# Two second key products in one PSUM bank, squared by one instruction

## The chip, the cores and the metric

The kernel runs on one core of one Trainium2 chip. The metric is the device time of one execution in microseconds (us). Five engines work side by side, each through its own queue in order: TensorE (PE in the profile; PEld are its weight loads), VectorE (DVE), ScalarE (ACT), GpSimd (POOL) and SyncE (SP, which issues DMAs). Engines wait for each other by semaphores only. Matmul results go to PSUM, which has eight banks of 512 fp32 values per partition; ACT and DVE read them there, POOL does not.

## The reference, cut to what matters

One inference step of a one-layer decoder: 1024 prompt tokens, and 8 sequences that decode 8 tokens each against a paged cache of 8192 positions. The change lies in the attention of the decoding tokens over the cached pages. For each page the cached latent `c` is projected to keys and values, and the keys are normalised per head:

```python
def latent_to_kv(ckv, krope, w_kvup, g_kn):
    kv = (ckv @ w_kvup).reshape(ckv.shape[:-1] + (MLA_HEADS, MLA_NOPE + MLA_V))
    k_nope = rmsnorm(kv[..., :MLA_NOPE], g_kn)
```

`rmsnorm` needs, for each cached position and each of the 8 heads, the sum of the squares of 64 key values. The scores, a running softmax over the pages and the sum over the values follow. Everything else of the layer (projections, gated linear attention, prompt attention, output projection, convolutional MLP, per-layer embedding) is "dense" work of the prompt.

## The kernel before, in words

**Cached pages.** Each sequence's 8192 positions are 8 blocks of 1024, so 64 blocks in all. A block is 8 tiles of 128 positions; the first block of a sequence has a ninth tile for the new tokens. `stage_load` (line 462) gathers a block by two indirect DMAs on POOL. `turn` (line 515) transposes four tiles on PE into one bank and splits them into a high and a low part on ACT (line 116) and DVE (line 117): `cTh`, `cTl`. A key is never kept: `main` (line 543) multiplies a tile by the key half of the projection only to get its squares, and the raw scores come from the same product, since the projection matrix `mv` carries 64 more columns with the query absorbed. `main` is called once per group of four tiles (and once for the ninth).

**The two products of a tile.** The 512 key columns and the 64 score columns don't fit one bank, so a tile has a first product of 320 columns (256 key columns, 64 scores) and a second of 256 columns. Each product is three fp32r matmuls (`mm3`, lines 138 to 141: high by high, high by low, low by high) into its own bank `ks` of the pool `psK`, which has three banks. ACT squares the 256 key columns out of the bank into `csq` (line 560) and, after a first product, copies the 64 scores to `sn` (line 562). When two tiles are squared, DVE sums their squares per head into `css` (line 565). The bank of a product is thus used again by the third product after it, once ACT has read it.

**What follows a block.** `stage_b` (line 580) turns the sums into inverse norms (ACT, DVE), scales the scores on POOL and takes their maxima; `stage_c1` (line 606) turns the maxima on PE (`mt`), takes exponentials on ACT and splits them into `phl`; `stage_pv` (line 638) multiplies them by the cached latents (`cpv`). These run one and two blocks behind `main`, as `cache_stream` (line 678) lays out: per block two steps, each ended by a `yield`.

**The order of the work.** The loop of lines 1602 to 1614 interleaves the cache stream with the dense work: each cache step is due 4.4 us times a factor `PACE` of the current dense part after the one before, each dense step names its own cost, and the one that is behind goes next. This gives the program order. From it, the queue of each engine is fixed when the program is built: the builder follows the program with its own estimates of durations and lets the first instruction in program order that it believes ready go next. What is estimated wrongly becomes a wait on the chip, with all that stands behind it in that queue. When the dense work has ended (`"fill" in z`), output-projection units (`wo_unit`, line 1424) are placed by hand between the pairs of tiles by `place` (line 574), and `behind` (line 570) keeps PE in program order there. The pool `psK` is closed after the cached pages; the MLP and the rest (from line 1616) don't use it.

Of the kernel before, what the change touches and what calls it, by code (L numbers as in the profile page):

```python
# [8 lines left out]
F32 = mybir.dt.float32  # L9
# [3 lines left out]
AF = mybir.ActivationFunctionType  # L13
ALU = mybir.AluOpType
AX = mybir.AxisListType
# [3 lines left out]
P = 128  # L19
# [26 lines left out]
def step_kernel(ctx: ExitStack, tc: tile.TileContext, A):  # L46
    nc = tc.nc
    pe, act, dve, pool, sp = nc.tensor, nc.scalar, nc.vector, nc.gpsimd, nc.sync
# [89 lines left out]
    def mm3(ps, ah, al, bh, bl, first=True, last=True):  # L138
        pe.matmul(ps, ah, bh, start=first, stop=False)  # L139
        pe.matmul(ps, ah, bl, start=False, stop=False)  # L140
        return pe.matmul(ps, al, bh, start=False, stop=last)  # L141
# [41 lines left out]
    psK = ph1.enter_context(tc.tile_pool(name="psK", bufs=3, space=PSUM))  # L183
    cp = ph1.enter_context(tc.tile_pool(name="cp", bufs=1, side="right"))
# [10 lines left out]
    def cst(shape, dt, name):  # L195
        return cp.tile(shape, dt, name=name, tag=name)

    oL = ctile([P, H, R], F32, "oTm")
    z = {}

    mv = [[cst([P, 576], F32R, f"mv{i}{s}") for s in "hl"] for i in range(2)]
# [341 lines left out]
    def main(o, g0):  # L543
        buf = o.b % 2
        if g0 == 0:
            o.sn = cp.tile([P, 9, 64], F32, tag="sn", name="sn", bufs=3)
            o.ss = cp.tile([P, 9, 8], F32, tag="css", name="css", bufs=2)
        gn = min(4, o.nt - g0)
        cTh, cTl = turned_c[groups.index((o.n, g0))]
        for i in range(gn):  # L550
            if i % 2 == 0:
                sq2 = cp.tile([P, 2, 512], F32, tag="csq", name="csq", bufs=2)
            sq = sq2[:, i % 2]
            for f in range(2):
                ks = psK.tile([P, 512], F32, tag="k", name="ks")
                w = 256 if f else 320
                mh, ml = (m[:, f * 320:f * 320 + w] for m in mv[buf])
                with behind():
                    z["chain"] = mm3(ks[:, :w], cTh[:, i, :], cTl[:, i, :], mh, ml).ins
                act.activation(sq[:, f * 256:f * 256 + 256], ks[:, 0:256], AF.Square)  # L560
                if f == 0:
                    act.copy(o.sn[:, g0 + i, :], ks[:, 256:320])  # L562
            if i % 2 or i == gn - 1:
                n = i % 2 + 1
                dve.tensor_reduce(o.ss[:, g0 + i + 1 - n:g0 + i + 1, :].rearrange("p i h -> p (i h)"),  # L565
                                  sq2[:, :n].rearrange("p i (h n) -> p (i h) n", n=64), AX.X, ALU.add)
                if "fill" in z and n == 2:
                    place()

    def behind():  # L570

        return tc.issue_after(z["chain"]) if "fill" in z and "chain" in z else nullcontext()

    def place():

        z["slot"] += 1
        if z["slot"] > 6 and z["slot"] % 8 and z["units"] < 49:
            fill(1)
# [99 lines left out]
    def cache_stream():  # L678
# [7 lines left out]
        for n in range(N + 2):  # L686
            z["block"] = n
            if n + 2 < N:
                blk[n + 2] = stage_load(*todo[n + 2], n + 2)
            if n < N:  # L690
                pre(blk, blk[n], 4)
                main(blk[n], 0)
            if 0 <= n - 2:
                stage_pv(blk[n - 2])
            if 0 <= n - 1 < N:
                stage_b(blk[n - 1])
            yield
            if n < N:
                if blk[n].nt == 9:
                    pre(blk, blk[n], 8)  # L700
                    main(blk[n], 4)
                    pre(blk, blk[n + 1], 0)
                    main(blk[n], 8)
                else:
                    if n + 1 < N:
                        pre(blk, blk[n + 1], 0)
                    main(blk[n], 4)
            if 0 <= n - 1 < N:
                stage_c1(blk[n - 1])
            if 0 <= n - 2:  # L710
                stage_c2(blk.pop(n - 2))
            yield
# [881 lines left out]
    def fill(n):  # L1594
        for _ in range(n):
            z["units"] += next(z["fill"], done) is None
# [5 lines left out]
    while live_c or live_d:  # L1602
# [4 lines left out]
        else:  # L1607
            w = next(dn, done)
# [268 lines left out]
    h, hs = z["h"], z["hs"]  # L1877
# [336 lines left out]
```

## Time and profile before

| what | us |
|---|---|
| time, median of three executions | 2253.16 |
| lowest, highest | 2251.01, 2255.33 |
| span of the profiled execution (first to last instruction) | 2250.3 |
| PE busy in it | 2147.8 (95%) |
| ACT busy | 1357.9 (60%) |
| DVE busy | 1681.4 (75%) |
| POOL busy | 1356.9 (60%) |

The profile is of one execution of its own; its time is told as its span, which leaves out what lies before the first and after the last instruction. A group's row reads: line, engine, operation, output<-input, shape, count, busy time, mean duration in ns, idle time of the engine just before these instructions and what ended it. A row of the waits reads: who waited, for whom, us in total, times, the longest. PE and PEld are one queue: a matmul's weight load goes ahead of it, so a product that waits for its bank shows as idle time before its weight load, its first matmul, or both.

### The profile page before, as it was taken

To read this page: it belongs to the slowest core of one execution; us is meant where nothing else is said; L and a number is where in the kernel's file an instruction comes from. 1 tells how busy PE (TensorE), PEld (TensorE's weight loads), DVE (VectorE), ACT (ScalarE), POOL (GpSimd) and SP (SyncE) were. 2 spreads that over 40 slices of the span, in tenths; PEclk is the share of its full clock that TensorE was granted. 3 is DMA by queue.
4 is the path that set the end of the run, shared out by engine and by line. 5 is a ranking of instruction groups with operands and counts; after the bars stand their busy time and mean duration, and the time that the engine had idled before them with its cause. 6 is when DMAs were issued, how large, how long until landed. Compare 5 with 4: busy or idle time off the path is not lost.

```text
span 2250.3 us, 38434 instructions
## 1 busy us (share of the span) xinstructions
PE 2147.8 (95%) x13459; PEld 1937.9 (86%) x13459; DVE 1681.4 (75%) x2490; ACT 1357.9 (60%) x3692; POOL 1356.9 (60%) x1395
## 2 busy tenths in 40 slices
PE   7999989999999999998999988999999999998999
PEld 6889978878888888887888867999999997786899
DVE  4675776467788888886978888888888877966632
ACT  5666766777778898886777775433333334334521
POOL 5675677577777777676455467656566643589000
PEclk9899999999999999999999998999999999999999
DMA  5343244413242222213322222322222228456321
GB/s 184 115 134 102 84 126 147 139 55 88 83 122 59 60 66 74 66 41 100 122 66 78 63 104 62 113 94 90 94 94 96 93 70 291 154 193 206 112 76 37
DMA packets 204547, 233.60 MB, mean 104 GB/s; under 512 B 42430, under 2 KB 146339, under 8 KB 204355
## 3 DMA queue, kind: packets, MB, share of 16 engines
q1 hardware_dynamic: 190691, 184.21, 26.1%
q0 software_dynamic: 12432, 42.48, 6.2%
q10 hardware_dynamic: 1232, 4.46, 0.5%
q8 instruction: 108, 1.77, 0.3%
q14 instruction: 84, 0.69, 0.1%
HBM read 188.52 MB, written 42.52 MB: 103 GB/s over the span
## 4 chain that ended last, share of the span: by engine, by line
PE 71%; DVE 9%; POOL 6%; DMA 5%; ACT 5%; issue 3%; SPq 0%; POOLq 0%; ACTq 0%; DVEq 0%
PE ps_gu L140 7%; PE ps_gu L141 7%; PE ps_gu L139 7%; PE ks L139 4%; PE ks L141 4%; PE ks L140 4%; PE cpv L645 2%; PE ctp L522 2%; DMA raw<-ffn_w_down 2%; PE ps_lt L278 2%; PE ps_pj L139 2%; DVE css L565 1%; PE ps_pj L140 1%; PE ps_pj L141 1%; PE ps_pg L140 1%
## 5 line engine op out<-in xcount | busy, mean ns | idle before, releaser
L560 ACT ACTIVATE csq<-ks 128x256 f32<-128x256 f32 x1040 | 392.4, 400 | 85.6 <-PE ks L141 76.6
L565 DVE TENSOR_REDUCE css<-csq 128x16 f32<-128x1024 f32 (+1 forms) x264 | 315.7, 1197 | 62.9 <-ACT csq L560 59.8
L116 ACT CAST wh<-st 128x512 fp32r<-128x512 f32 x176 | 108.3, 619 | 183.3 <-PE ps_gu L140 163.8
L139 PE MATMUL ks<-mv1h,cTh 128*128 128x320 f32 (+1 forms) x520 | 169.5, 328 | 8.4 <-ACT sn L562 3.6
L139 PE MATMUL ks<-mv0h,cTh 128*128 128x320 f32 (+1 forms) x520 | 170.8, 330 | 6.9 <-ACT csq L560 3.0
L604 POOL TENSOR_TENSOR chl<-craw,chl 128x1024 fp32r<-128x1024 f32 x64 | 141.2, 2206 | 57.3 <-ACT chl L603 56.7
L140 PE MATMUL ks<-mv1l,cTh 128*128 128x320 f32 (+1 forms) x520 | 153.3, 297 | 0.0
L140 PE MATMUL ks<-mv0l,cTh 128*128 128x320 f32 (+1 forms) x520 | 152.1, 294 | 0.0
L141 PE MATMUL ks<-mv0h,cTl 128*128 128x320 f32 (+1 forms) x520 | 147.8, 297 | 0.9 <-DVE cTl L117 0.8
L630 POOL TENSOR_TENSOR phl<-sn,phl 128x512 fp32r<-128x512 f32 (+1 forms) x64 | 84.8, 1326 | 105.0 <-ACT phl L629 104.6
L141 PE MATMUL ks<-mv1h,cTl 128*128 128x320 f32 (+1 forms) x520 | 147.9, 298 | 0.0
L117 DVE TENSOR_TENSOR wl<-st,wh 128x512 fp32r<-128x512 f32 x132 | 119.0, 903 | 29.0 <-ACT wh L116 29.0
L140 PE MATMUL ps_dn<-o 128*128 128x512 f32 x308 | 125.6, 408 | 12.1 <-DVE o L117 12.0
L117 POOL TENSOR_TENSOR wl<-st,wh 128x512 fp32r<-128x512 f32 x44 | 69.1, 1574 | 104.3 <-ACT wh L116 104.3
L139 PE MATMUL ps_dn<-o 128*128 128x512 f32 x308 | 119.6, 399 | 4.5 <-ACT o L116 4.5
L141 PE MATMUL ps_dn<-o 128*128 128x512 f32 x308 | 123.8, 402 | 0.0
L117 DVE TENSOR_TENSOR cTl<-ctp,cTh 128x512 fp32r<-128x512 f32 (+1 forms) x136 | 90.0, 662 | 37.3 <-ACT cTh L116 36.3
L1317 POOL TENSOR_TENSOR pl<-p,ph 128x512 fp32r<-128x512 f32 (+1 forms) x96 | 97.4, 1019 | 33.0 <-DVE ph L1316 23.2
L562 ACT COPY sn<-ks 128x64 f32<-128x64 f32 x520 | 117.1, 225 | 0.0
L139 PEld LDWEIGHTS ks<-mv1h,cTh 128*128 128x128 f32 x520 | 98.8, 190 | 20.7 <-ACT sn L562 7.4
L139 PEld LDWEIGHTS ks<-mv0h,cTh 128*128 128x128 f32 x520 | 97.9, 188 | 20.8 <-ACT sn L562 7.0
L139 PE MATMUL ps_gu<-xrh,wh 128*128 128x320 f32 x352 | 108.6, 309 | 0.9 <-ACT xrh L116 0.9
(675 smaller groups left out, 8019.0 us busy)
## 6 DMA issues: line engine op xcount, KB each, us to landing
raw<-ds SPq DMA_DIRECT2D x77, 256.0 KB
raw<-ffn_w_down SPq DMA_DIRECT2D x66, 256.0 KB
stage<-w_in SPq DMA_DIRECT2D x48, 256.0 KB
st<-ffn_w_gate SPq DMA_DIRECT2D x44, 256.0 KB
st<-ffn_w_up SPq DMA_DIRECT2D x44, 256.0 KB
wr<-ffn_w_down SPq DMA_DIRECT2D x44, 256.0 KB
ds<-cv SPq DMA_DIRECT2D x21, 512.0 KB
oraw<-doT SPq DMA_DIRECT2D x16, 256.0 KB
```

The costliest lines, as they stand in the source:

```text
L116: act.copy(hi, src)
L117: (lo_eng or dve).tensor_tensor(lo, src, hi.bitcast(F32), ALU.subtract)
L139: pe.matmul(ps, ah, bh, start=first, stop=False)
L140: pe.matmul(ps, ah, bl, start=False, stop=False)
L141: return pe.matmul(ps, al, bh, start=False, stop=last)
L278: pe.matmul(ps, x, w, start=first, stop=last)
L560: act.activation(sq[:, f * 256:f * 256 + 256], ks[:, 0:256], AF.Square)
L562: act.copy(o.sn[:, g0 + i, :], ks[:, 256:320])
L565: dve.tensor_reduce(o.ss[:, g0 + i + 1 - n:g0 + i + 1, :].rearrange("p i h -> p (i h)"), sq2[:, :n].rearrange("p i (h n) -> p (i h) n", n= ...
L604: pool.tensor_tensor(ch[:, c0:c1, 128:256], src, ch[:, c0:c1, 0:128].bitcast(F32), ALU.subtract)
L630: pool.tensor_tensor(phl[:, :nt, 64:128], sb, phl[:, :nt, 0:64].bitcast(F32), ALU.subtract)
L1317: pool.tensor_tensor(pl[:, c0:], p[:, c0:], ph[:, c0:].bitcast(F32), ALU.subtract)
```

## The change

The second products of two neighbouring tiles go into the two halves of one bank (`ks2`, shape 128x2x256, same pool and tag, so still three banks in all), and one ACT instruction squares both halves (512 columns) into the two tiles' parts of `csq`. First products keep a bank each, with their square and copy. The order of a pair becomes: first product of tile i, first product of tile i+1, second product of tile i, second product of tile i+1. The ninth tile stands alone, with n = 1. The reduction on DVE and the call of `place` come after the pair as before.

```diff
-        for i in range(gn):
-            if i % 2 == 0:
-                sq2 = cp.tile([P, 2, 512], F32, tag="csq", name="csq", bufs=2)
-            sq = sq2[:, i % 2]
-            for f in range(2):
+        def product(ks, i, f, w):
+            mh, ml = (m[:, f * 320:f * 320 + w] for m in mv[buf])
+            with behind():
+                z["chain"] = mm3(ks, cTh[:, i, :], cTl[:, i, :], mh, ml).ins
+
+        for i in range(0, gn, 2):
+            n = min(2, gn - i)
+            sq2 = cp.tile([P, 2, 512], F32, tag="csq", name="csq", bufs=2)
+            for e in range(n):
                 ks = psK.tile([P, 512], F32, tag="k", name="ks")
-                w = 256 if f else 320
-                mh, ml = (m[:, f * 320:f * 320 + w] for m in mv[buf])
-                with behind():
-                    z["chain"] = mm3(ks[:, :w], cTh[:, i, :], cTl[:, i, :], mh, ml).ins
-                act.activation(sq[:, f * 256:f * 256 + 256], ks[:, 0:256], AF.Square)
-                if f == 0:
-                    act.copy(o.sn[:, g0 + i, :], ks[:, 256:320])
-            if i % 2 or i == gn - 1:
-                n = i % 2 + 1
-                dve.tensor_reduce(o.ss[:, g0 + i + 1 - n:g0 + i + 1, :].rearrange("p i h -> p (i h)"),
-                                  sq2[:, :n].rearrange("p i (h n) -> p (i h) n", n=64), AX.X, ALU.add)
-                if "fill" in z and n == 2:
-                    place()
+                product(ks[:, :320], i + e, 0, 320)
+                act.activation(sq2[:, e, 0:256], ks[:, 0:256], AF.Square)
+                act.copy(o.sn[:, g0 + i + e, :], ks[:, 256:320])
+            ks = psK.tile([P, 2, 256], F32, tag="k", name="ks2")
+            for e in range(n):
+                product(ks[:, e], i + e, 1, 256)
+            act.activation(sq2[:, :n, 256:512], ks[:, :n], AF.Square)
+            dve.tensor_reduce(o.ss[:, g0 + i:g0 + i + n, :].rearrange("p i h -> p (i h)"),
+                              sq2[:, :n].rearrange("p i (h n) -> p (i h) n", n=64), AX.X, ALU.add)
+            if "fill" in z and n == 2:
+                place()
```

## The prediction

> **What bounds the kernel now.** I read the page first: the span, the busy shares and the chain of work that ended last.
>
> ```profile
> span 2250.3 us, 38434 instructions
> PE 2147.8 (95%) x13459; PEld 1937.9 (86%) x13459; DVE 1681.4 (75%) x2490; ACT 1357.9 (60%) x3692; POOL 1356.9 (60%) x1395
> ...
> PE   7999989999999999998999988999999999998999
> ...
> ACT  5666766777778898886777775433333334334521
> ...
> PE 71%; DVE 9%; POOL 6%; DMA 5%; ACT 5%; issue 3%; SPq 0%; POOLq 0%; ACTq 0%; DVEq 0%
> ```
>
> PE is the bound nearly everywhere. ACT, from which the change takes work, has 5% of the chain; in its fourteenth to eighteenth slice (731 to 1013 us) it is 80 to over 90% busy, so there its queue can make PE wait. The change touches only the stretch of the cached pages, 75 to 1306 us. The windows view of that stretch, first of all instructions and then of those on `ks`; its columns are the length, busy time of each engine with counts, granted clock and DMA:
>
> ```profile
> 75.00:1306.00 1231.00, 1183.83 (x7903) 1044.73 (x7902) 936.07 (x1535) 947.32 (x2925) 812.78 (x881) 0.99 0.30 89
> ```
>
> ```profile
> 75.00:1306.00 1231.00, 545.98 (x3115) 448.51 (x3113) 421.36 (x1560) 0.99 0.30 89
> ```
>
> PE is idle for 1231.0 - 1183.8 = 47.2 us of it. ACT is busy for 947 us (77%), and 421 us of that reads `ks`. So ACT's busy time bounds nothing; a gain must come out of PE's waits, or out of the start cost of its matmuls. The waits view, first of PE alone over the span, then of the stretch:
>
> ```profile
> PE ks L139 <- ACT sn L562: 6.4, 14, 1.6
> ...
> PE ks L139 <- ACT csq L560: 5.0, 7, 1.4
> ...
> PE mt L616 <- POOL ml L599: 2.7, 3, 1.9
> ...
> PE cpv L645 <- POOL phl L630: 1.6, 3, 1.2
> ```
>
> ```profile
> ACT csq L560 <- PE ks L141: 76.6, 103, 3.5
> ...
> PEld ks L139 <- ACT sn L562: 14.4, 30, 1.9
> ...
> PEld ks L139 <- ACT csq L560: 8.6, 15, 1.6
> ...
> PEld ks L139 <- ACT cTh L116: 5.3, 9, 1.4
> ```
>
> A product that waits for ACT's copy `sn` or square `csq` waits for its bank: that is what the change can shorten. It is 6.4 + 5.0 = 11.4 us seen at the matmuls, 14.4 + 8.6 = 23.0 us seen at the weight loads. They are one queue, and some of it is counted in both: the cost lies between 11.4 and 34.4 us. I take 23, since the weight load is what a product begins with.
>
> **Part 1: ACT's squares.** 520 tiles are 256 pairs and 8 single tiles. Of 1040 squares of 256 columns, 512 go and 256 of 512 columns come; the 520 copies stay. The rows by shape:
>
> ```profile
> L560 ACT ACTIVATE csq<-ks 128x256 f32<-128x256 f32 x1040 | 392.4, 400 | 85.6 <-PE ks L141 76.6 <-DVE css L565 2.9 <-PE csr L141 0.3
> ...
> L603 ACT CAST chl<-craw 128x1024 fp32r<-128x1024 f32 x64 | 67.7, 1057 | 27.9 <-PE cpv L645 11.4 <-issue 8.1 <-POOL sn L594 3.8
> ...
> L510 ACT COPY sr<-csr 128x512 f32<-128x512 f32 x64 | 38.7, 604 | 16.5 <-PE csr L141 12.7 <-POOL sn L594 1.6 <-POOL rs_r L112 1.0
> ```
>
> By durations: 512 x 0.400 - 256 x 0.604 = 204.8 - 154.6 = 50 us less on ACT. When ACT's instructions follow each other they overlap, as this timeline shows (start, duration):
>
> ```profile
> 1225.22 0.38 ACT L560 ACTIVATE csq<-ks 128x256 f32<-128x256 f32 x1 [0.45 <-PE ks L141]
> ...
> 1225.50 0.21 ACT L562 COPY sn<-ks 128x64 f32<-128x64 f32 x1
> ...
> 1225.59 0.40 ACT L560 ACTIVATE csq<-ks 128x256 f32<-128x256 f32 x1
> ```
>
> The copy starts 0.28 us after the square, and the next square 0.09 us after the copy: each hides about 0.10 to 0.12 us of itself. Then a square of 256 costs 0.28 and one of 512 about 0.604 - 0.12 = 0.48, and the saving is 256 x (0.56 - 0.48) = 20 us. So ACT is relieved by 20 to 50 us of 947. The page "ScalarE: Activation LUTs" of the Trainium skill (What ACT_TABLE_LOAD costs) gives 186 ns + 0.833 ns a column and an overlap of 93 ns; by it, an estimate, two squares of 256 less one of 512 are 93 ns, or 24 us over 256 pairs. The rows agree (400, 604, 0.10 to 0.12). Since ACT isn't the bound, the relief alone is worth only its share of PE's other waits for ACT: 2 to 5% of the 5.3 us for `cTh`. I count it as nothing.
>
> **Part 2: PE's matmuls.** The same twelve matmuls a pair, with the same operands; no instruction is added or removed on PE, DVE, POOL or SP, and no DMA. Only the order inside a pair and the target change. Two products side by side in one bank occur already, in `ps_gv`:
>
> ```profile
> L139 PE MATMUL ks<-mv0h,cTh 128*128 128x256 f32 x260 | 82.4, 317 | 3.0 <-ACT sn L562 2.8
> ...
> L140 PE MATMUL ks<-mv0l,cTh 128*128 128x256 f32 x260 | 72.7, 280 | 0.0
> ...
> L139 PE MATMUL ps_gv<-w,xTh 128*128 128x256 f32 x128 | 37.2, 291 | 0.0
> L140 PE MATMUL ps_gv<-w,xTh 128*128 128x256 f32 x128 | 36.7, 287 | 0.0
> ```
>
> A shared bank costs PE at most 287 - 280 = 7 ns a matmul, x 1536 = 11 us if all of it were the bank's; it may be nothing, since `ps_gv` differs in neighbours too. I take nothing. The first matmul of a second product takes 317 against 280 for the next: a start cost. The pair's last product needs no bank of its own, and saves at most 256 x 37 ns = 9.5 us. Most of that cost stands behind transposes and other causes that stay, so I take 45 waits x 37 ns = 2 us.
>
> **Part 3: the bank waits.** The step from start to start is 0.15 us for 320 columns and 0.12 for 256:
>
> ```profile
> 1221.19 0.31 PE L140 MATMUL ks<-mv1l,cTh 128*128 128x320 f32 x1
> ...
> 1221.34 0.31 PE L141 MATMUL ks<-mv1h,cTl 128*128 128x320 f32 x1
> ...
> 1221.48 0.28 PE L139 MATMUL ks<-mv1h,cTh 128*128 128x256 f32 x1
> ...
> 1221.60 0.28 PE L140 MATMUL ks<-mv1l,cTh 128*128 128x256 f32 x1
> ```
>
> So a first product is 0.45 us and a second 0.36. Now a bank is wanted again two products after its end: 0.45 + 0.36 = 0.81 us, while ACT needs 0.40 (square), or 0.40 + 0.21 = 0.61 with the copy. Any longer instruction that ACT has in between, as `chl` with 1.06 us, makes PE wait, 0.51 us on average (23.0 over 45). After the change a first product's bank is wanted again after a first product and a double one: 0.45 + 0.72 = 1.17 us, for the same 0.61 of reading; 0.36 us more room. The double bank is wanted after two first products, 0.90 us, for 0.60: its slack falls from 0.81 - 0.40 = 0.41 to 0.30, but there are half as many. The waits for `sn` (30 of 0.48 us) keep 0.12 us each, 3.6 us; those for `csq` (15 of 0.57) become some 8 of 0.68, 5.4 us. Left are 9 of 23 us: a gain of 14 us. Bounds: nothing (PE only waits elsewhere) and 23 + 9.5 us.
>
> **Part 4: the later end of a pair.** The square of the first of the two second products now starts up to 0.36 us later, and the pair's last square ends 0.20 us later (0.60 against 0.40), so `css` is late by 0.2 us. What follows on DVE and ACT feeds `mt` and `cpv` on PE half a block and more later (1231 us / 64 = 19 us a block), and PE waited there 3 + 3 times in the rows above. This cover hides it but for 6 x 0.2 = 1.2 us; bare it would be 64 x 0.2 = 13 us. I take 1 us.
>
> **Sum** on the profiled span: 2250.3 - 2 - 14 + 1 = 2235.3 if PE's gain is passed on whole. The rest of PE's 47.2 us of idle time has other causes (DVE, POOL), and some of what is won is waited for there: I keep three quarters, 11 us. The three runs lie 0.7 to 5.0 us above the span, their median 2.9: 2239 + 3 = 2242 us, 0.5% below the median. The new order of the queues also redraws the other 36 us of PE's waits; a quarter of them, 9 us, is my width to either side: 2233 to 2251.
>
> **Rivals.** *The wait moves (0.2).* PE's bank waits go, but the same PE time is waited for at DVE's and POOL's results: 76% and 66% busy in the stretch, and `mt` and `cpv` waits stand in the rows. For it speaks that only 11.4 us of the bank waits show as idle matmul time. Time: 2253 - 2, 2251.
>
> *The double square blocks ACT (0.3), slower.* ACT takes its queue in order. The single square can't start before both products have ended, and behind it in the queue stand the `cTh` casts, `chl` and the exponentials, for which PE and POOL wait. Now 103 of 1040 squares find PE unfinished, for 76.6 us. A pair's square has to wait for 0.36 us more of PE and then runs 0.20 longer: 0.56 us for every pair that ACT reaches early. PE's queue now waits for ACT's results on `ks` and `cTh` for 23.0 + 5.3 = 28.3 us against those 76.6 us, 0.37 of it. At 0.56 x 0.37 = 0.21 us a pair the gain of 11 us is spent at 52 of the 256 pairs; with 110 early pairs the kernel is 12 us slower, 2265. Against it: a tenth of the squares finds PE unfinished now, which would be 26 pairs. It decides where dense matmuls stand between the two second products, which stretches the wait from 0.36 us to microseconds. The page "PSUM — Partial Sum Buffer" of the Trainium skill (Summary: rules for kernel authors) says that a bank should be read while matmuls write a different one, guarded bank by bank: by that rule the first half can't be read early, which is this rival. No run here shows what ignoring it would do.
>
> *It doesn't do what it says (0.03).* If the square of 512 cost 0.80, ACT would save nothing; the row of 604 speaks against it. The time would be the wait-moves case.
>
> **How the numbers follow.** The forecast's case has 0.47, the others 0.2, 0.3 and 0.03. A measurement of this kernel can tell about 0.2%, 4.5 us. Faster by more takes 0.40 of the forecast's case, 0.06 of the cases at 2251 and 0.01 of the slower one: 0.47. Within takes 0.05, 0.14 and 0.02: 0.21. Slower takes 0.02, 0.03 and 0.27: 0.32. The likeliest case's own range is 2233 to 2251; to hold 8 in 10 it must reach into the slower rival: 2233 to 2265.
>
> **What would show it.** Right: 784 squares on L560 and its successor, 528 of 256 columns and 256 of 512 at about 0.60 us; ACT's time on `ks` down from 421 us to between 371 and 401; bank waits of `ks` at the weight loads near 9 us instead of 23.0; PE's idle time in the stretch near 36 us and the end of the `ks` work some 11 us earlier; nothing different after it. Wrong: ACT's idle time before the squares well above 76.6 us with more PE waits for `cTh` or `kTh` (blocking square), bank waits gone but `mt`, `cpv` or `S` waits grown (moved wait), or 512-column squares well above 0.60 us.

## The result, and the profile after

The changed kernel took 2290.65 us, the median of runs between 2289.15 and 2294.14; the kernel before, run beside it, took 2252.09 (2248.33 to 2255.33). The ratio is 1.0174 [1.0158, 1.0190]: slower by 1.7%, where 2242 us and a gain of 0.5% had been forecast, and beyond the upper end of the range, 2265. The profiled execution's span grew by 38.9 us.

The page of the changed kernel, cut to lines that answer to those of before:

```profile
span 2289.2 us, 38036 instructions
PE 2153.9 (94%) x13459; PEld 1948.9 (85%) x13459; DVE 1697.7 (74%) x2490; ACT 1343.7 (59%) x3436; POOL 1358.2 (59%) x1395
...
PE 72%; DVE 12%; DMA 5%; ACT 4%; POOL 4%; issue 3%; SPq 1%; DVEq 0%; ACTq 0%; POOLq 0%
```

PE does the same 13459 matmuls. ACT is busy 14 us less and has 4% of the chain instead of 5%. DVE, from which and to which nothing was moved, has 12% of it instead of 9%. The mean granted clock of the execution, from the view of the cores (before, then after):

```profile
core 0: 2250.3 us, clock 0.980
```

```profile
core 0: 2289.2 us, clock 0.972
```

The clock in these records is 1.00 or about 0.50, so the time at half clock is about 2 x (1 - clock) x span: 90 us before, 128 after.

The windows view of the stretch of the cached pages, which now ends at 1340 us instead of 1306 (columns as in the prediction: length, busy time of PE, PEld, DVE, ACT and POOL with counts, clock, DMA), of all instructions and of those on `ks`:

```profile
75.00:1340.00 1265.00, 1196.80 (x7921) 1061.67 (x7920) 945.08 (x1538) 933.38 (x2672) 812.69 (x887) 0.97 0.29 87
```

```profile
75.00:1340.00 1265.00, 525.10 (x3120) 452.31 (x3120) 389.01 (x1304) 0.97 0.29 87
```

The stretch is 34 us longer, but not all of that lies in the work on the cached pages: the first product on `ks` starts at 74.1 us before and at 78.6 after, though up to there PE's queue is the same in both. (Two more kernels with the changed kernel's queues, e7 and e8 below, start it at 73.4 and 75.9 us, so these 4.5 us are scatter.) The same view from the first product to the last, before and then after:

```profile
74.10:1305.20 1231.10, 1183.93 (x7906) 1045.01 (x7905) 936.05 (x1536) 947.20 (x2926) 813.48 (x883) 0.99 0.30 90
```

```profile
78.60:1338.80 1260.20, 1191.99 (x7898) 1057.83 (x7897) 943.51 (x1536) 931.18 (x2667) 810.19 (x879) 0.97 0.29 87
```

This is 29.1 us longer. PE is idle for 1260.2 - 1192.0 = 68.2 us of it, 21.0 more than before, and busy for 8.1 us more with 8 fewer matmuls, since more of them ran at half clock. The other 9.8 us of the 38.9 are the 4.5 at the start and 5.3 after the cached pages, where the queues were redrawn too.

The groups by shape in this stretch (mean ns of one, idle time before):

```profile
L567 DVE TENSOR_REDUCE css<-csq 128x16 f32<-128x1024 f32 x256 | 310.7, 1214 | 99.3 <-ACT csq L566 98.2
L561 ACT ACTIVATE csq<-ks 128x256 f32<-128x256 f32 x520 | 204.5, 400 | 65.7 <-PE ks L141 64.0 <-DVE css L567 0.3
L566 ACT ACTIVATE csq<-ks 128x512 f32<-128x512 f32 x256 | 159.1, 622 | 29.5 <-PE ks L141 28.4
...
L139 PE MATMUL ks<-mv0h,cTh 128*128 128x256 f32 x260 | 78.1, 300 | 0.5 <-ACT csq L566 0.4
...
L140 PE MATMUL ks<-mv0l,cTh 128*128 128x256 f32 x260 | 74.1, 285 | 0.0
```

The squares are what the change says, the double ones at 622 ns. The first matmul of a second product takes 300 ns instead of 317, the next ones 285 instead of 280. The 5 ns belong to the half clock and not to the bank: of the matmuls more than 1 us away from any half clock, those next ones take 280 ns on average in both kernels. So sharing a bank costs PE's matmuls nothing that can be seen.

The waits of PE's weight loads over the span, after, and then of before the two rows that the prediction didn't show (us in total, times, longest):

```profile
PEld csr L141 <- DVE kTl L117: 12.6, 10, 4.2
PEld ks L139 <- ACT cTh L116: 10.5, 15, 1.9
...
PEld ks L141 <- DVE cTl L117: 8.2, 8, 3.8
...
PEld ks L139 <- ACT sn L562: 4.6, 7, 1.4
...
PEld ks L139 <- ACT csq L566: 3.4, 8, 0.9
```

```profile
PEld ks L141 <- DVE cTl L117: 1.8, 3, 1.0
PEld csr L141 <- DVE kTl L117: 1.7, 1, 1.7
```

Here is the turn. The bank waits (`sn`, `csq`) fell from 23.0 to 8.0 us. The waits for operands, the turned cache tiles `cTh` and `cTl` and the turned rope keys `kTl`, rose: 5.3 to 10.5, 1.8 to 8.2 and 1.7 to 12.6. With `kTh`, which fell from 2.6 to 0.8, they are 11.4 us before and 32.2 after.

One of the stalls, in the chain of waits of the changed kernel between 136 and 145 us (start, duration, what):

```profile
135.57 1.21 DVE css L567
136.78 4.84 DVE kt L945
141.62 0.60 DVE qt L327
142.22 0.33 DVE qt L330
142.55 0.33 DVE qss L318
142.88 0.19 DVE qss L319
143.08 0.34 DVE kTl L117
143.42 0.04 issue
143.46 0.39 PE csr L141
```

`kTl` itself takes DVE 0.34 us, but it stands in DVE's queue behind a sum of squares and five instructions of the dense work, of which one, `kt`, takes 4.84 us. PE waits for 4.01 us. The windows view of the two sides of that stall, during it and after it:

```profile
139.30:143.40 4.10, 0.15 (x2) 0.00 (x0) 4.10 (x7) 0.29 (x1) 3.93 (x4) 1.00 0.23 84
143.80:147.20 3.40, 3.40 (x14) 2.74 (x13) 2.92 (x8) 2.30 (x7) 2.20 (x4) 0.51 0.97 254
```

For 3.4 us after the stall the granted clock is 0.51. The timeline of PE shows what that costs: the same `ps_gv` matmuls start 0.21 us apart at first and 0.12 us apart at the end.

```profile
146.05 0.41 PE L139 MATMUL ps_gv<-w,xTh 128*128 128x256 f32 x1
146.26 0.41 PE L140 MATMUL ps_gv<-w,xTh 128*128 128x256 f32 x1
...
147.66 0.28 PE L139 MATMUL ps_gv<-w,xTh 128*128 128x256 f32 x1
147.78 0.27 PE L140 MATMUL ps_gv<-w,xTh 128*128 128x256 f32 x1
```

### The profile page after: what moved, and what is told of

Same layout as the page of the kernel before. It is cut to its first block, busy times and chain, and to the rows that moved or that the text cites. A ratio compares the mean times of both kernels' runs of the same rounds, so it can differ in the third digit from the quotient of the medians.

```text
span 2289.2 us, 38036 instructions
## 1 busy us (share of the span) xinstructions
PE 2153.9 (94%) x13459; PEld 1948.9 (85%) x13459; DVE 1697.7 (74%) x2490; ACT 1343.7 (59%) x3436; POOL 1358.2 (59%) x1395
## 4 chain that ended last, share of the span: by engine, by line
PE 72%; DVE 12%; DMA 5%; ACT 4%; POOL 4%; issue 3%; SPq 1%; DVEq 0%; ACTq 0%; POOLq 0%
PE ps_gu L141 7%; PE ps_gu L139 7%; PE ps_gu L140 7%; PE ks L139 5%; PE ks L141 5%; PE ks L140 5%; PE cpv L647 2%; PE ctp L522 2%; DVE o L117 2%; PE ps_lt L278 2%; PE ps_pj L139 2%; PE ps_pj L141 1%; PE ps_pj L140 1%; DMA raw<-ffn_w_down 1%; PE ps_pg L140 1%
## 5 line engine op out<-in xcount | busy, mean ns | idle before, releaser
L567 DVE TENSOR_REDUCE css<-csq 128x16 f32<-128x1024 f32 (+1 forms) x264 | 316.1, 1198 | 100.9 <-ACT csq L566 99.8
L561 ACT ACTIVATE csq<-ks 128x256 f32<-128x256 f32 x520 | 204.5, 400 | 65.7 <-PE ks L141 64.0
L566 ACT ACTIVATE csq<-ks 128x512 f32<-128x512 f32 (+1 forms) x264 | 162.5, 616 | 29.6 <-PE ks L141 28.4
L139 PE MATMUL ks<-mv1h,cTh 128*128 128x320 f32 (+1 forms) x520 | 164.2, 317 | 3.1 <-ACT cTh L116 1.4
L594 POOL TENSOR_TENSOR sn<-sn,cy 128x512 f32<-128x512 f32 (+1 forms) x64 | 71.4, 1115 | 68.3 <-DVE cy L592 55.5
```

What stands on the lines that cost most here:

```text
L561: act.activation(sq2[:, e, 0:256], ks[:, 0:256], AF.Square)
L566: act.activation(sq2[:, :n, 256:512], ks[:, :n], AF.Square)
L567: dve.tensor_reduce(o.ss[:, g0 + i:g0 + i + n, :].rearrange("p i h -> p (i h)"), sq2[:, :n].rearrange("p i (h n) -> p (i h) n", n=64), AX. ...
```

## Experiments

The theory tested first was that the kernel lost by its queues: a redrawn plan, and, in that plan, operands that come too late. Its rival was the prediction's own: that the double square holds ACT, and all that stands behind it, until both products have ended. The changed kernel differs from the one before in three things that can be had separately: the order of the products in a pair, the shared bank, and the merged square. Beside these, every edit redraws the queues, since the builder places instructions by its own estimates. So every variant but the control e12 was also built with the pace of the cache stream changed by 1%, which changes no work and redraws much of the queues: between the kernel before and its twin at 1.01, 5974 of PE's 13459 positions hold another instruction. In the table, the ratio is to the kernel before on the same chip. Bank waits and operand waits are sums of rows of the waits view as above (weight loads on the cached pages), with all other waits of weight loads longer than 0.15 us beside them, from the first product to the last. (Idle time that the view puts down to `issue`, to no other engine and no DMA, is left out; it is 33 to 37 us in every kernel.) The clock is that of the profiled execution.

| kernel | pace | us | ratio [95%] | bank | operands | other | clock |
|---|---|---|---|---|---|---|---|
| before | 1.00 | 2252.09 | 1 | 23.2 | 11.4 | 45.7 | 0.980 |
| before (e3) | 1.01 | 2265.19 | 1.0057 [1.0037, 1.0077] | 26.0 | 10.1 | 57.0 | 0.979 |
| before (e4) | 0.99 | 2263.24 | 1.0059 [1.0039, 1.0079] | 22.1 | 17.3 | 46.8 | 0.979 |
| new order only (e1) | 1.00 | 2282.57 | 1.0140 [1.0123, 1.0157] | 21.6 | 21.0 | 59.3 | 0.977 |
| new order only (e15) | 1.01 | 2271.59 | 1.0088 [1.0071, 1.0105] | 19.2 | 14.3 | 62.6 | 0.976 |
| new order only (e16) | 0.99 | 2267.38 | 1.0069 [1.0052, 1.0087] | 21.7 | 10.8 | 65.6 | 0.980 |
| shared bank, two squares (e2) | 1.00 | 2265.23 | 1.0058 [1.0041, 1.0074] | 13.9 | 18.8 | 53.8 | 0.974 |
| shared bank, two squares (e9) | 1.01 | 2275.52 | 1.0110 [1.0088, 1.0133] | 12.6 | 23.8 | 66.7 | 0.982 |
| shared bank, two squares (e10) | 0.99 | 2278.47 | 1.0108 [1.0086, 1.0131] | 10.1 | 22.4 | 73.2 | 0.972 |
| changed | 1.00 | 2290.65 | 1.0174 [1.0158, 1.0190] | 8.0 | 32.2 | 61.5 | 0.972 |
| changed (e5) | 1.01 | 2285.80 | 1.0140 [1.0123, 1.0156] | 8.1 | 35.2 | 67.7 | 0.978 |
| changed (e6) | 0.99 | 2304.21 | 1.0220 [1.0203, 1.0237] | 6.7 | 38.7 | 70.5 | 0.971 |
| changed, late rope products (e11) | 1.00 | 2261.76 | 1.0040 [1.0026, 1.0055] | 7.7 | 22.1 | 61.1 | 0.979 |
| changed, late rope products (e13) | 1.01 | 2277.39 | 1.0114 [1.0091, 1.0137] | 9.1 | 18.1 | 69.3 | 0.976 |
| changed, late rope products (e14) | 0.99 | 2260.85 | 1.0038 [1.0024, 1.0052] | 8.8 | 19.8 | 60.4 | 0.976 |
| before, late rope products (e12) | 1.00 | 2270.96 | 1.0079 [1.0062, 1.0095] | 22.2 | 10.3 | 63.3 | 0.978 |

### The three parts of the change, taken apart

**The order alone.** Against the changed kernel, every second product has a bank and a square of its own again:

```diff
-            ks = psK.tile([P, 2, 256], F32, tag="k", name="ks2")
             for e in range(n):
-                product(ks[:, e], i + e, 1, 256)
-            act.activation(sq2[:, :n, 256:512], ks[:, :n], AF.Square)
+                ks = psK.tile([P, 512], F32, tag="k", name="ks2")
+                product(ks[:, :256], i + e, 1, 256)
+                act.activation(sq2[:, e, 256:512], ks[:, 0:256], AF.Square)
```

> Only the new order of a pair's products (first, first, second, second); every product has its own bank and its own square, as before. Blocking (the one square that stands for two products holds up ACT and DVE, and PE then waits for the low parts kTl and cTl): the loss of 38 us goes for the most part, 2250 to 2262 us, and PE's waits for kTl and cTl fall from 21 us to below 10. Order (the new order of the products itself): 2280 to 2295. Redrawn queues (any new plan of the queues is worse than the one it was paced for): anywhere from 2260 to 2295, and no nearer to one kernel than to the other.

Measured: 1.0140, with none of the double squares, inside the range of "order"; `kTl` and `cTl` together were waited for 15 us. Bank waits stayed at 21.6 us. Most of the changed kernel's loss seemed to be in the order; the plans at another pace, below, took much of that back.

**The shared bank with two squares.** Against the changed kernel:

```diff
-            act.activation(sq2[:, :n, 256:512], ks[:, :n], AF.Square)
+            for e in range(n):
+                act.activation(sq2[:, e, 256:512], ks[:, e], AF.Square)
```

> The new order and the shared bank, but its two halves are squared by two instructions of 256 columns, both after both products. Blocking: as slow as the changed kernel or slower, 2285 to 2300, since the squares still wait for both products. Merged instruction (the square of 512 columns itself): 2250 to 2262. Redrawn queues: anywhere from 2260 to 2295.

Measured: 1.0058, above the range of "merged instruction" and below that of "blocking"; only the wide range of "redrawn queues" holds it. It holds the same products in the same banks as the changed kernel, and is 25 us faster. Its waits at the weight loads:

```profile
PEld ks L139 <- ACT cTh L116: 8.7, 15, 2.2
...
PEld ks L139 <- ACT sn L562: 7.5, 13, 2.0
...
PEld ks L139 <- ACT csq L567: 6.4, 11, 1.0
...
PEld ks L141 <- DVE cTl L117: 4.8, 8, 1.6
...
PEld csr L141 <- DVE kTl L117: 1.6, 2, 1.4
```

The bank waits are 13.9 us, `cTh` and `cTl` are late as in the changed kernel, but `kTl` is hardly ever: 2 waits for 1.6 us, against 10 for 12.6.

### What a redrawn plan costs by itself

```diff
-            due += 4.4 * PACE[z["part"]]
+            due += 4.4 * 1.01 * PACE[z["part"]]
```

(or 0.99). In the kernel before:

> The kernel before, with the cache steps due 1% later (4.4 us times 1.01); the work is the same, only the program order and so the plan of the queues changes. Blocking and order: 2247 to 2260, within 0.4% of before. Redrawn queues: 2262 to 2295, a loss of 10 to 40 us from the plan alone.

> The kernel before, with the cache steps due 1% earlier (4.4 us times 0.99). Blocking and order: 2247 to 2260. Redrawn queues: 2262 to 2295.

Measured: 1.0057 and 1.0059. In both, a redrawn plan with the old work is some 13 us slower, most of it PE's idle time: 57.0 and 55.2 us of the stretch instead of 47.2. In the changed kernel:

> The changed kernel with the cache steps due 1% later: the same work, another plan of the queues. The pace of the kernel before cost 13 and 15 us when it was moved by 1% either way, so a plan alone is worth that much. Redrawn queues: the changed kernel's loss is the luck of one plan, so this one lands at 2255 to 2280. Sharing (the shared bank and the one square are slower in themselves): 2284 to 2305, no better than the changed kernel.

> The changed kernel with the cache steps due 1% earlier. Redrawn queues: 2255 to 2280. Sharing: 2284 to 2305. If one of the two nudges lands low and the other high, the plan decides by itself.

Measured: 1.0140 and 1.0220. No pace gets it near the kernel before, and the plan at 0.99 is the worst of all. Its waits at the weight loads:

```profile
PEld csr L141 <- DVE kTl L117: 16.7, 10, 5.1
PEld ks L139 <- ACT cTh L116: 12.9, 18, 0.9
...
PEld ks L141 <- DVE cTl L117: 6.1, 10, 2.3
...
PEld ks L139 <- ACT sn L562: 3.6, 10, 1.2
...
PEld ks L139 <- ACT csq L566: 3.1, 7, 0.9
```

It has the fewest bank waits of all the kernels, 6.7 us, and the most operand waits, 38.7. The two-squares variant and the new order alone, at both paces:

> Shared bank with two squares of 256, cache steps due 1% later. The kernel before lies at 2250, 2265 and 2263 over three plans, the changed one at 2290, 2286 and 2304. Merged square (it is the one instruction of 512 that costs): shared bank with two squares stays with before, 2258 to 2272. Sharing (the bank that waits for two products costs, and the single run at 2265 was a lucky plan): 2278 to 2300.

> The same, cache steps due 1% earlier. Merged square: 2258 to 2272. Sharing: 2278 to 2300.

> The new order of products alone, own banks and squares, cache steps due 1% later; at the unchanged pace it took 2283. New order: 2275 to 2295, so the order of the products is slow in itself. Redrawn queues: 2255 to 2270, as the kernel before takes when its pace is moved.

> The same, cache steps due 1% earlier. New order: 2275 to 2295. Redrawn queues: 2255 to 2270.

Measured: 1.0110 and 1.0108, 1.0088 and 1.0069. Three of the four lie between the two ranges that had been expected, or at the edge of one; so neither expectation can be read off a single plan. Means over the three plans are then: before 0.4% (0 to 0.6), new order 1.0% (0.7 to 1.4), shared bank with two squares 0.9% (0.6 to 1.1), changed 1.8% (1.4 to 2.2). The mean of before holds the one plan to which the pace was fitted. Against its two redrawn plans, 0.6%, the new order costs about 0.4% more, which three plans that scatter by 0.7% don't make sure; sharing the bank costs nothing more, and the merged square about 0.9%, some 20 us. That last step is the clearest: the lowest of the changed plans lies above the highest with two squares, though their intervals still touch. Within a variant, one plan differs from another by 0.5 to 0.8%, so no single plan could have told these steps apart.

### Two edits that changed nothing

The splits that make `cTh`, `cTl`, `kTh` and `kTl` were given a higher rank in the builder, and, in another kernel, the sum of squares on DVE was put later in the program:

```diff
-        split(kTh[:, :n * P], kTl[:, :n * P], rp[:, :n * P])
+        with tc.high_priority(SP):
+            split(kTh[:, :n * P], kTl[:, :n * P], rp[:, :n * P])
...
-        split(cTh[:, :gn], cTl[:, :gn], tp[:, :gn])
+        with tc.high_priority(SP):
+            split(cTh[:, :gn], cTl[:, :gn], tp[:, :gn])
```

> The changed kernel, with the splits that make cTh, cTl, kTh and kTl ranked 50 places earlier when the queues are planned. Late low parts (PE, freed of its bank waits, reaches the products before DVE has made cTl and kTl, which stand behind dense work in DVE's queue): PE's waits for cTl and kTl fall from 21 us to below 8 and the time to 2260 to 2275. Redrawn queues: the waits fall but others take their place, 2270 to 2295.

```diff
+            summed_up()
             ks = psK.tile([P, 2, 256], F32, tag="k", name="ks2")
...
-            dve.tensor_reduce(o.ss[:, g0 + i:g0 + i + n, :].rearrange("p i h -> p (i h)"),
-                              sq2[:, :n].rearrange("p i (h n) -> p (i h) n", n=64), AX.X, ALU.add)
+            held.append((sq2, i, n))
```

(`summed_up` does the reductions held so far, once more at the end of the group.)

> The changed kernel, with the reduction of a group's first pair put after the first products of its second pair in program order, so that DVE comes to it when the square of 512 has ended. Blocking (the reduction waits for the one square and holds up DVE's queue): DVE's idle time before the reductions falls from 100 us to below 60 and the time to 2255 to 2275. If DVE's queue isn't held up by the reductions but by dense work: the idle time may fall, the time stays at 2275 to 2300.

Measured: 1.0192 [1.0164, 1.0220] and 1.0173 [1.0156, 1.0190]. Neither says anything on its theory: on PE, DVE, ACT and POOL both kernels hold the same instructions in the same order as the changed one, position by position. In the builder's plan, neither edit moved anything. They are two repeats of the changed kernel, and show how far one plan scatters: 2294.5 and 2294.3 us beside 2290.7, operand waits of 32.9 and 33.3 us beside 32.2.

### Giving the rope keys more time

In the changed kernel, and then in the kernel before, the rope products into `csr` were moved behind the key products of the first four tiles of their block, so that `kTl` has that long to arrive. This moves instructions, so it redraws the queues as well:

```diff
         split(kTh[:, :n * P], kTl[:, :n * P], rp[:, :n * P])
+        o.late = lambda: rope_products(o, g0, n, kTh, kTl)
+
+    def rope_products(o, g0, n, kTh, kTl):
...
                 main(blk[n], 0)
+                blk[n].late()
```

> The changed kernel; the rope scores of a block (the matmuls into csr, which need kTl from DVE) come after the products of the block's first half in program order and not ahead of them; same work. Late operands (PE, no longer held at the banks, comes to products whose low or high part isn't made yet): PE's waits for kTl fall from 12.6 us to below 3, half-clock time and span fall with them, 2265 to 2280. Lump (the squares come late and in lumps to DVE): the waits for kTl move to cTl and cTh, 2283 to 2300.

> The kernel before with the same move, as a control: its waits for kTl are 2 us already, so late operands gives 2250 to 2265 (what any new plan gives), lump the same.

Measured: 1.0040 for the changed kernel with it, 29 us less than without, and 1.0079 for the kernel before with it, 18 us more than without. The first is faster than either case had foreseen (2265 at best), with more `kTl` waits left than the 3 us of its case; the second lies above its range, 2250 to 2265. The weight-load waits of the first:

```profile
PEld ks L139 <- ACT cTh L116: 8.0, 14, 1.8
...
PEld ks L141 <- DVE cTl L117: 7.1, 5, 4.8
...
PEld ks L139 <- ACT sn L566: 4.6, 11, 1.4
...
PEld csr L139 <- DVE kTl L117: 2.8, 3, 2.3
...
PEld csr L141 <- DVE kTl L117: 0.6, 1, 0.6
```

The `kTl` waits go from 12.6 us to some 5 in all (these rows 3.4), the other operands from 19.6 to 16.8, PE's idle time in the stretch goes from 68.2 to 55.3 us and the clock is 0.979 again. At the other paces:

> The changed kernel with the late rope products, cache steps due 1% later. The changed kernel over three plans: 2290, 2286, 2304; with late rope products 2262 once. Late operands: the move is worth its 30 us whatever the plan, 2255 to 2275, with kTl waits below 6 us. Luck (the one plan was good): 2280 to 2305.

> The same, cache steps due 1% earlier. Late operands: 2255 to 2275. Luck: 2280 to 2305.

Measured: 1.0114 and 1.0038; the first is just above the range of "late operands", 2255 to 2275. Over three plans the edit takes 1.1%, some 26 us, off the changed kernel, about what the merged square had cost. It is still slower than before in all three. The gain isn't the `kTl` waits alone: plan by plan they fall by 7.3, 4.2 and 15.2 us, the time by 29, 8 and 43. The other waits and the half clock changed with the redrawn queues too.

## Why the prediction was wrong, point by point

**Part 1 was right.** There are 784 squares. ACT's time on `ks` fell from 421.4 to 389.0 us, 32 us, inside the 20 to 50, and a double square took 622 ns for the 604 foreseen. ACT's relief was counted as nothing, and nothing of it can be seen in the time.

**Part 2 was right in kind and too low in size.** Sharing a bank cost the matmuls nothing visible. The first matmul of a second product took 17 ns less on average; over 520 that is 9 us, near the bound of 9.5 and not the 2 us that were taken. Matmul durations overlap, so not all of it need be time.

**Part 3's mechanism and its total were right.** 9 us of bank waits were foreseen at the weight loads, 8.0 were measured, and 6.7 to 9.2 in all eight kernels with the merged square. How the total is made up was not foreseen: instead of 30 waits of 0.12 us for `sn` there were 7 of 0.66, and instead of 8 of 0.68 for `csq` 8 of 0.43. The agreement of the total is in part luck.

**Part 4** can't be read apart from the rest. The sum of squares waited more for its square (59.8 us before, then 99.8):

```profile
DVE css L565 <- ACT csq L560: 59.8, 76, 4.7
```

```profile
DVE css L567 <- ACT csq L566: 99.8, 110, 4.5
```

The same wait is 90 to 97 us in the three plans with two squares, so it comes with the shared bank and not with the merged instruction.

**The sum failed**, in its step "I keep three quarters, 11 us". It expected PE to keep three quarters of what it won at the banks; PE kept nothing, and its idle time, which should have fallen by 11 us, rose by 21.0. The waits for operands and for other results rose by more than the bank waits fell. The account of all weight-load waits in the stretch over 0.15 us is: bank waits -15.2, operand waits +20.8, all others +15.8, together +21.4 us, close to the 21.0 of idle time. So the gain at the banks was more than given back at the operands alone. The prediction had such a row (5.3 us for `cTh`), but set a quarter of the gain aside for all other waits together, without asking who makes the operands and how early they are ready. `kTl` and `cTl` come from DVE, in a queue in which dense work stands ahead of them, as the stall at 139 us shows.

**The width failed too.** "A quarter of them, 9 us, is my width to either side" treated a redrawn plan as a draw that can fall either way. None of the 15 redrawn plans that ran, the changed kernel's among them, was faster than before; the two that only redraw it are some 13 us slower. The pace of the kernel before fits its own queues, so a redraw is a cost, of about 0.6% in these two, and not a width around zero. In the other waits the redraw is seen: 45.7 us before, 46.8 to 73.2 in all others.

**The clock was left out.** PE's 8 us of additional busy time go with more time at half clock, 75 us between the first and the last product instead of 31: many of the added stalls are followed by a few us of it. Over the 18 profiles a least-squares fit gives the length of the stretch, from the first product to the last, as 1175 us + 0.97 x PE's idle time + 0.27 x the time at half clock, within 6 us: an idle us costs a whole us, and what is clocked down after it is added.

**The rivals.** "The wait moves" names what happened in kind: the waits at `cpv` for `phl` rose too (from 2.8 to 7.8 us at the weight loads, over the span), those at `mt` hardly, but most of it moved to operands that it didn't name, and it doesn't end at 2251, since a moved wait need not be of the same size. "The double square blocks ACT" foresaw the sign, and both of its marks are there. ACT's idle time for PE ahead of squares is 64.0 + 28.4 = 92.4 us for 76.6 (rows by shape above); but the new order alone, without a double square, has 97.6 us there, and the two redrawn plans of the kernel before 82 and 88, so this mark says little. The second, more PE waits for `cTh`, holds better: 4 to 7 us in the plans of before and of the new order, 9 to 13 in all with the shared bank and the rope products in their old place, with two squares (8.8, 11.1, 11.9) as with one (10.5, 9.0, 12.9). So some blocking in ACT's queue agrees with the traces, but it comes with the shared bank, whose plans are no slower than the new order, and it isn't what sets the changed kernel apart. That is `kTl`, from DVE: 12.6, 7.3 and 16.7 us, against 1.6, 2.2 and 2.5 with two squares. The same double squares with late rope products cost 0.4%, 1.1% and 0.4%, no more on average than two squares do in the early place (two squares with late rope products weren't run). This speaks for the merged square not being dear where it runs, but in the plans that come with it. That those plans meet a late `kTl` was shown, and that moving its user takes these waits and most of the loss away; how much of that is `kTl` and how much the redrawn queues wasn't separated.

**What stays open** is why the plans with the merged square put `csr` where `kTl` is late and those with two squares don't. That DVE's blocked sum of squares holds up `kTl` was meant to be tried by the later sum, whose queues came out unchanged. The traces speak against it as the whole cause: the sums wait for their squares as long with two squares (90 to 97 us), where `kTl` is hardly late, as with one (85 to 108). Turning the cache tiles one group further ahead would give `cTh` and `cTl` more time, but needs a third buffer for them; it wasn't tried.

## What to carry to other kernels

Before counting a removed wait as gained, look at what the waiting engine needs next and how early that is ready: a wait can be given back with interest one instruction later, where the operand's maker has a queue of its own. Where a builder places the queues and a pace was fitted to them, price a redrawn plan as a cost, and measure it with an edit that changes no work. Judge a variant over several plans, because here one plan differed from another of the same kernel by about as much as the parts of the change.

## What the runs showed of the hardware

A short stall of PE can be enough for half clock. In the changed kernel PE's rope product waits 1.57 us, and the windows view of the wait and of what follows shows the clock (its column stands third from the end):

```profile
477.33 0.30 PE L141 MATMUL csr<-qbd0h,kTl 128*128 128x64 f32 x1 [1.57 <-DVE kTl L117]
```

```profile
475.80:477.30 1.50, 0.00 (x0) 0.00 (x0) 1.46 (x5) 0.18 (x1) 1.50 (x3) 1.00 0.01 1
478.30:485.10 6.80, 6.80 (x34) 6.26 (x32) 1.58 (x4) 3.37 (x14) 4.97 (x6) 0.50 0.45 137
```

PE is busy without a gap for 6.8 us at a clock of 0.50, after a stall of a quarter of that. It doesn't always follow: after a stall of 1.64 us at 489 us the clock stays at 1.00.

```profile
489.20:490.90 1.70, 0.06 (x2) 0.03 (x1) 1.43 (x3) 1.70 (x5) 0.00 (x0) 1.00 0.00 0
490.90:508.30 17.40, 15.89 (x110) 13.37 (x110) 15.34 (x27) 13.34 (x42) 9.63 (x12) 1.00 0.23 70
```

In all 18 profiles together, half clock began during the stall or within 3.5 us after it in 52 of the 132 stalls of 1.5 to 2 us that started at full clock, and in all 67 that were longer than 3.5 us. The page "TensorE: Matmul & The Clock Gate" of the Trainium skill (Part 1: The HAM clock gate) has the rate halved after an idle window of some 3.4 us, in windows that run freely. The trace agrees on the half rate and on the lengths, 3.4 and 6.8 us; that the stall must itself be 3.4 us long it doesn't bear out.

In the stall at 139 us, DVE's normalisation `kt` took 4.92 us, beside a subtraction on POOL (timeline of the changed kernel; the three `w` parts are one row):

```profile
136.71 4.92 DVE L945 TENSOR_TENSOR kt<-kt,rs_r 128x512 f32<-128x512 f32 x1
...
137.32 3.74 POOL L117 TENSOR_TENSOR w<-stage,w 128x512 fp32r<-128x512 f32 x3
```

Over its eight instances it took 694 ns at least, 2006 at the median and 6553 at most (before: 674, 1480 and 1783). The page "SBUF — State Buffer" of the Trainium skill (Who interferes with whom) says that a DVE instruction with two inputs in SBUF contends with a GpSimd instruction that reads SBUF. The spread of the durations agrees with that; no run here took the POOL instruction away, so the cause is argued and not shown.
